# A pair of token tiles closed together, memory rows scaled on GpSimd, and a score reduction moved in its queue: one edit to a two-layer decoder trunk

## The chip, the cores and the metric

The kernel runs on one core of one Trainium2 chip. A core has five engines that each work through a queue of their own in order: TensorE (PE in the profile; PEld is its weight load), VectorE (DVE), ScalarE (ACT), GpSimd (POOL) and SyncE (SP, which here only issues DMAs). The metric is the time of one execution in microseconds: 1540.67 us before (median of three runs, 1540.62 to 1540.80).

## The reference

Two decoder layers over 512 tokens of 1024 channels, all in float32:

```
for l in range(2):
    a = hybrid_mixer(rms_norm(x, pre_mix_g[l]), ...)   # 8 latent (MLA) heads + 8 dilated-window heads
    x = x + rms_norm(a, post_mix_g[l])
    c = memory_cross_attention(rms_norm(x, pre_xattn_g[l]), rms_norm(mem, mem_g[l]), ...)
    x = x + rms_norm(c, post_xattn_g[l])
    h = square(relu(rms_norm(x, pre_mlp_g[l]) @ w_up[l]))
    x = x + rms_norm(h @ w_down[l], post_mlp_g[l])
```

`rms_norm(x, g)` is `x * rsqrt(mean(x*x) + 1e-6) * g` over a row. `mem` is 256 rows of 1024 channels, the same for both layers; the cross attention has 4 heads of 256 channels, the MLP 4096 hidden channels. Softmaxes are causal (latent heads), banded with a bias (dilated heads) or full (memory).

## The kernel before, in words

Tokens lie in four tiles of 128 rows (t = 0 to 3), channels in two halves of 512 (n = 0, 1). `xs[t][n]` is the residual stream. A float32 factor is split into a high part (on ACT) and a low part (on DVE, the difference), and each product is three matmuls: low times high, high times low, high times high (lines 247 to 249). The weights come by DMA into `raw` and are split into `whi` (line 193) and `wlo` (line 199).

A row norm takes four steps on four engines: ACT squares a half and adds it up (`sumsq`, "junk" is its unused output), DVE adds both halves' sums and EPS (a 128x1 tile, `...m`), POOL raises it to the power -1/2 (`rpow`, line 139, `...r`), and then the rows are scaled. For a sub-layer's output (`add_post_norm`, `pnm` and `pnr`) DVE does the last step together with the residual addition (line 432). For the next sub-layer's input (`norm_x`, `n1m` and `n1r` at the layer boundary) POOL scales half 0 into `xn` (line 417) and ACT half 1 (line 414); PE then transposes `xn` through PSUM tiles `tp`, and the result is split into `xth` and `xtl` (line 205).

The order on each engine is made by a scheduler when the program is built: it takes the program order as priorities, and `tc.issue_after(x)` places an instruction behind another. Generators for attention, latent projections and memory work are woven into one stream (`weave`); transposes are put off (`put_off`) so that matmuls can go in front. An instruction that waits holds up all that stands behind it on its engine.

Four places matter here.

- Attention start of a layer. `ev_kd` splits the keys of the dilated heads into `kh` (ACT) and `kl` (DVE, line 663); POOL copies both to the other half of the partitions. `scores` computes a head's scores in four widths, 128 to 512: PE writes `sp`, DVE adds the bias and takes the row minimum into `nm` (line 485), ACT takes the exponent (line 489), POOL divides by the sum (line 491). There are two `sp` buffers, so a third width waits for the reduction of the first. While `pinned[0]` is set, PE's score matmuls are kept in program order, and the first exponent of a head stands behind the last `kh`.
- Memory norm (`memory_norm`): the rows of `mem` (`mr[t][n]`, two tiles of two halves) are normed per tile t, with the scaling on DVE (line 835). It is one of the fills beside the attention heads, once in each layer. PE transposes `mr` later.
- Layer boundary. The MLP's second product runs over seven combinations of quarter matrices (`plan`, as in Winograd's form of Strassen's method); `wa`, `wc` and `we` are their PSUM results, added to `acc[t][n]`. Token tiles 0 and 1 are complete after the fifth combination of the last quarter, tiles 2 and 3 after the last. `done` then takes the sum of squares (`junkp`), multiplies by the gain `gb`, and after a tile's second half calls `add_post_norm` and `norm_x`.
- End of the program. In the last layer tiles 0 and 1 are closed by `finish_by_transfer`: `acc` is scaled (line 1081), a DMA that POOL issues adds the residual `xmid` to it, and SP stores it. Tiles 2 and 3 go through `add_post_norm`, whose `xs` is stored by SP and ACT.

## Time and profile before

| | |
|---|---|
| median of three runs | 1540.67 us (1540.62 to 1540.80) |
| profiled execution | 1540.44 us |
| its span in the trace | 1538.6 us |
| TensorE busy | 1501.9 us, 98% |
| VectorE busy | 985.1 us, 64% |
| ScalarE busy | 821.0 us, 53% |
| GpSimd busy | 253.9 us, 16% |
| chain that ended last | 83% PE, 9% DVE, 3% ACT, 3% issue, 1% POOL |

The span is what the trace covers; 1.8 us of the profiled execution lie outside it. Busy time is summed over an engine's instructions; an engine's idle time costs something only where another engine's end depends on it.

### The profile page before, as it was taken

What the parts mean: (1) busy time and instruction counts of PE and PEld (TensorE: products, weight loads), DVE (VectorE), ACT (ScalarE), POOL (GpSimd) and SP (SyncE); (2) the same over time, 40 slices, a digit from 0 to 9 for tenths busy, and PEclk for the clock granted to TensorE, in tenths of its full rate; (3) what the DMA queues carried; (4) which work ended last, traced back from release to release, by engine and by line L of the source; (5) the groups of instructions that cost most, each with busy time, mean ns of one, the idle gap of its engine ahead of it and who ended that gap; (6) DMA issues with size and microseconds to landing.
All of it is one profiled execution on the core that took longest, in us unless ns stands there. A gap on an engine that the chain in (4) does not pass through costs nothing.

```text
span 1538.6 us, 21318 instructions
## 1 busy us (share of the span) xinstructions
PE 1501.9 (98%) x7861; PEld 1261.4 (82%) x7861; DVE 985.1 (64%) x1768; ACT 821.0 (53%) x1578; POOL 253.9 (16%) x441
## 2 busy tenths in 40 slices
PE   9989999999999999999989999999999999999997
PEld 7777788898898888888868877978988988888885
DVE  5556865456459677684964667654654594958667
ACT  5356665355357364645644666654553654546363
POOL 2143621021020000000111455201111100000002
PEclk9999999999999999999999999999999999999999
DMA  6423223513131505153642322243322324060535
GB/s 235 153 81 105 87 78 103 186 56 123 55 110 56 178 28 182 38 175 97 201 121 64 117 93 73 69 151 137 110 83 69 113 72 158 15 191 28 181 85 117
DMA packets 89581, 168.29 MB, mean 109 GB/s; under 512 B 6358, under 2 KB 12164, under 8 KB 89476
## 3 DMA queue, kind: packets, MB, share of 16 engines
q1 hardware_dynamic: 86436, 161.15, 32.6%
q0 software_dynamic: 2752, 5.24, 2.1%
q8 instruction: 62, 1.02, 0.3%
q10 hardware_dynamic: 288, 0.52, 0.1%
q14 instruction: 43, 0.35, 0.1%
HBM read 158.49 MB, written 11.03 MB: 110 GB/s over the span
## 4 chain that ended last, share of the span: by engine, by line
PE 83%; DVE 9%; ACT 3%; issue 3%; POOL 1%; DMA 1%; SPq 0%; DVEq 0%; POOLq 0%; ACTq 0%
PE pfm L248 12%; PE pfm L247 12%; PE pfm L249 12%; PE ptm L247 6%; PE ptm L249 6%; PE ptm L248 6%; PE wa L247 3%; PE wa L248 3%; PE wa L249 3%; PE sp L481 3%; PE op L238 3%; DVE wlo L199 2%; PE ptp L230 2%; PE wc L248 1%; PE wc L247 1%
## 5 line engine op out<-in xcount | busy, mean ns | idle before, releaser
L248 PE MATMUL pfm<-xth,wlo 128*128 128x512 f32 (+1 forms) x896 | 322.4, 360 | 0.6
L247 PE MATMUL pfm<-xtl,whi 128*128 128x512 f32 (+1 forms) x896 | 322.2, 360 | 0.0
L249 PE MATMUL pfm<-xth,whi 128*128 128x512 f32 (+1 forms) x896 | 321.6, 359 | 0.0
L199 DVE SCALAR_TENSOR_TENSOR wlo<-raw,gT,whi 128x512 fp32r<-128x512 f32 (+3 forms) x332 | 229.5, 728 | 125.1 <-ACT whi L193 123.5
L193 ACT ACTIVATE whi<-raw,gT 128x512 fp32r<-128x512 f32 (+2 forms) x324 | 209.6, 697 | 174.0 <-PE pfm L249 87.3
L248 PEld LDWEIGHTS pfm<-xth,wlo 128*128 128x128 f32 x896 | 169.1, 189 | 26.9 <-DVE wlo L199 1.4
L249 PEld LDWEIGHTS pfm<-xth,whi 128*128 128x128 f32 x896 | 169.1, 189 | 25.5 <-issue 0.5
L247 PEld LDWEIGHTS pfm<-xtl,whi 128*128 128x128 f32 x896 | 169.2, 189 | 25.0
L164 ACT ACTIVATE whi<-raw 128x1024 fp32r<-128x1024 f32 x112 | 118.1, 1059 | 130.5 <-PE pfm L249 54.0
L165 DVE TENSOR_TENSOR wlo<-raw,whi 128x1024 fp32r<-128x1024 f32 x112 | 134.7, 1219 | 39.1 <-ACT whi L164 39.1
L1068 POOL DMA_DIRECT2D raw<-in_w_down x8 | 9.8, 1230 | 596.2 <-DVE raw L1071 540.1
L491 POOL TENSOR_SCALAR P<-P,rs 128x128 f32<-128x128 f32 (+3 forms) x128 | 73.3, 578 | 156.2 <-DVE rs L490 66.6
L247 PE MATMUL wa<-wlo,fh 128*128 128x512 f32 x240 | 93.6, 390 | 0.5 <-DVE acc L1153 0.5
L248 PE MATMUL wa<-whi,fl 128*128 128x512 f32 x240 | 93.4, 389 | 0.0
L249 PE MATMUL wa<-whi,fh 128*128 128x512 f32 x240 | 93.4, 389 | 0.0
L489 ACT ACTIVATE P<-P,nm 128x128 f32<-128x128 f32 (+3 forms) x128 | 71.2, 557 | 24.6 <-DVE nm L485 23.9
L185 DVE TENSOR_TENSOR wlo<-raw,whi 128x1024 fp32r<-128x1024 f32 x32 | 39.1, 1222 | 59.4 <-ACT whi L184 58.6
L247 PE MATMUL ptm<-wlo,xth 128*128 128x512 f32 (+2 forms) x192 | 68.4, 357 | 5.2 <-DVE wlo L199 4.4
L184 ACT ACTIVATE whi<-raw 128x1024 fp32r<-128x1024 f32 x32 | 33.9, 1061 | 67.3 <-PE ptm L249 60.2
L1071 DVE TENSOR_TENSOR raw<-raw 128x1024 f32<-128x1024 f32 x56 | 67.8, 1217 | 0.2
L248 PE MATMUL ptm<-whi,xtl 128*128 128x512 f32 (+2 forms) x192 | 66.5, 346 | 0.2 <-DVE xtl L205 0.2
L249 PE MATMUL ptm<-whi,xth 128*128 128x512 f32 (+2 forms) x192 | 66.5, 346 | 0.0
(253 smaller groups left out, 3257.8 us busy)
## 6 DMA issues: line engine op xcount, KB each, us to landing
raw<-in_w_up SPq DMA_DIRECT2D x64, 512.0 KB, 4.6
raw<-in_w_down SPq DMA_DIRECT2D x64, 512.0 KB, 4.2
raw<-in_w_in SPq DMA_DIRECT2D x24, 512.0 KB, 5.6
raw<-in_w_xk SPq DMA_DIRECT2D x16, 512.0 KB, 4.1
raw<-in_w_xv SPq DMA_DIRECT2D x16, 512.0 KB, 3.7
raw<-in_w_mix_out SPq DMA_DIRECT2D x16, 512.0 KB, 4.1
raw<-in_w_xq SPq DMA_DIRECT2D x16, 512.0 KB, 6.2
raw<-in_w_xo SPq DMA_DIRECT2D x16, 512.0 KB, 3.6
```

The lines of the kernel that those rows point to most:

```text
L164: nc.scalar.activation(hi, raw, AF.Copy)
L165: nc.vector.tensor_sub(lo, raw, hi.bitcast(F32))
L193: weight_parts[:] = [nc.scalar.activation(cols(hi, k, False), cols(raw, k, True), AF.Copy, scale=g).ins]
L199: nc.vector.scalar_tensor_tensor(lv, rv, g, hv, op0=OP.mult, op1=OP.subtract)
L238: nc.tensor.matmul(ps, lhsT=lhsT, rhs=rhs, start=start, stop=stop)
L247: in_order(nc.tensor.matmul(ps, lhsT=lh, rhs=rl, start=first, stop=False, skip_group_check=more))
L248: in_order(nc.tensor.matmul(ps, lhsT=ll, rhs=rh, start=False, stop=False, skip_group_check=more))
L249: in_order(nc.tensor.matmul(ps, lhsT=lh, rhs=rh, start=False, stop=last, skip_group_check=more))
L481: in_order(nc.tensor.matmul(sp[:, :L], lhsT=q[:, i * 128:(i + 1) * 128], rhs=k[:, :L], start=n == 0, stop=n == len(parts) - 1))
L489: nc.scalar.activation(Pi, Pi, AF.Exp, bias=nm[:, i:i + 1], scale=-1.0, accum_out=rs[:, i:i + 1])
L491: nc.gpsimd.tensor_scalar(Pi, Pi, rs[:, i:i + 1], 1.0, op0=OP.mult, op1=OP.mult)
L1071: nc.vector.tensor_add(tile_, tile_, more)
```

## The change

It does four things.

1. The first score reduction of layer 0's first head (DVE) is issued behind the last `kl` subtraction, as the first exponent already was behind the last `kh`.
2. `pinned[0]` is set in layer 0 only; in layer 1 the scheduler orders the attention start freely.
3. The memory norm has one DVE addition (128x2) and one power (128x2) for both tiles, and the four scalings of `mr` go from DVE to POOL.
4. `close_pair` closes tiles 0 and 1 together, once both are complete: one `pnm`, one power, and in layer 0 the four residual additions, one `n1m` and `n1r`, and for each tile one scaling on POOL and one on ACT. In layer 1 it has one power, four scalings of `acc` and the four adding DMAs and stores.

```diff
-    last_key = [None]
+    last_key = [None, None]
...
-            score_op[0] = nc.vector.tensor_tensor_reduce(
-                out=Pi, in0=sp[:, :L], in1=tb[:, 512 - L:512], scale=-scale, scalar=3e38, op0=OP.add,
-                op1=OP.min, accum_out=nm[:, i:i + 1]).ins
+            with tc.issue_after(last_key[1]) if pinned[0] and i == 0 else nullcontext():
+                score_op[0] = nc.vector.tensor_tensor_reduce(
+                    out=Pi, in0=sp[:, :L], in1=tb[:, 512 - L:512], scale=-scale, scalar=3e38, op0=OP.add,
+                    op1=OP.min, accum_out=nm[:, i:i + 1]).ins
...
-                    nc.vector.tensor_sub(lo[here, :], ps[here, :], u[here, :].bitcast(F32))
+                    last_key[1] = nc.vector.tensor_sub(lo[here, :], ps[here, :], u[here, :].bitcast(F32)).ins
...
+            ms = small("mms", 4)
             for t in range(2):
-                ms = small("mms", 2)
                 for n in range(2):
-                    sumsq(mr[t][n], ms[:, n:n + 1], scale=1.0 / 32.0)
-                r = row_rstd((ms[:, 0:1], ms[:, 1:2]), "nm")
+                    sumsq(mr[t][n], ms[:, 2 * n + t:2 * n + t + 1], scale=1.0 / 32.0)
+                yield
+            m = small("nmm", 2)
+            nc.vector.scalar_tensor_tensor(m, ms[:, 0:2], EPS, ms[:, 2:4], op0=OP.add, op1=OP.add)
+            r = rpow(m, "nm")
+            for t in range(2):
                 for n in range(2):
-                    nc.vector.tensor_scalar(mr[t][n], mr[t][n], r[:, 0:1], None, op0=OP.mult)
+                    nc.gpsimd.tensor_scalar(mr[t][n], mr[t][n], r[:, t:t + 1], 1.0, op0=OP.mult, op1=OP.mult)
                 yield
...
-        pinned[0] = True
+        pinned[0] = l == 0
...
-        def finish_by_transfer(t):
-            m = small("pnm", 1)
-            ...
+        def close_pair():
+            v = pair_ss.rearrange("p (t n) -> p t n", t=2)
+            m = small("pnm", 2)
+            nc.vector.scalar_tensor_tensor(m, v[:, :, 0], EPS, v[:, :, 1], op0=OP.add, op1=OP.add)
             r = rpow(m, "pn")
+            if l == DEPTH - 1:
+                for t in range(2):
+                    for n in range(2):
+                        rows, cols = slice(t * 128, (t + 1) * 128), slice(n * 512, (n + 1) * 512)
+                        nc.vector.scalar_tensor_tensor(acc[t][n], acc[t][n], r[:, t:t + 1], gb[n], op0=OP.mult,
+                                                       op1=OP.mult)
+                        nc.gpsimd.dma_start(acc[t][n], xmid[rows, cols], accum_op=OP.add)
+                        nc.sync.dma_start(out[0, rows, cols], acc[t][n])
+                return
+            ms = small("n1ms", 4)
+            for t in range(2):
+                for n in range(2):
+                    nc.vector.scalar_tensor_tensor(xs[t][n], acc[t][n], r[:, t:t + 1], xs[t][n], op0=OP.mult,
+                                                   op1=OP.add)
+                    sumsq(xs[t][n], ms[:, 2 * t + n:2 * t + n + 1], scale=1.0 / 32.0)
+                store_x(t, xsave)
+            v = ms.rearrange("p (t n) -> p t n", t=2)
+            m = small("n1m", 2)
+            nc.vector.scalar_tensor_tensor(m, v[:, :, 0], EPS, v[:, :, 1], op0=OP.add, op1=OP.add)
+            r = rpow(m, "n1")
+            ...
+            for t in range(2):
+                xns = [unit("xn") for _ in range(2)]
+                nc.gpsimd.tensor_scalar(xns[0], xs[t][0], r[:, t:t + 1], 1.0, op0=OP.mult, op1=OP.mult)
+                nc.scalar.activation(xns[1], xs[t][1], AF.Copy, scale=r[:, t:t + 1])
+                put_off(("xt", t), DELAY, lambda t=t, xns=xns: [
+                    transposed(xns[n], n, list(zip(hv, lv)), t) for n in range(2)])
...
-            if ready_halves[t] < 2:
+            if ready_halves[t] < 2 or t == 0:
                 return
-            if by_transfer:
-                finish_by_transfer(t)
+            if t == 1:
+                close_pair()
                 return
```

The order of instructions moves with it. The first place is DVE at layer 0's attention start. Before:

```order
L663 TENSOR_TENSOR kl<-pfm,kh 64x512 x3
L485 ISA P,nm<-sp,tb 128x128
L485 ISA nm 128x1
L663 TENSOR_TENSOR kl<-pfm,kh 64x512 x3
L199 SCALAR_TENSOR_TENSOR wlo<-raw,gT,whi 128x288
L663 TENSOR_TENSOR kl<-pfm,kh 64x512
L199 SCALAR_TENSOR_TENSOR wlo<-raw,gT,whi 128x288 x3
L663 TENSOR_TENSOR kl<-pfm,kh 64x512
L485 ISA P,nm<-sp,tb 128x256
L485 ISA nm 128x1
L485 ISA P,nm<-sp,tb 128x384
```

In the changed kernel:

```order
L664 TENSOR_TENSOR kl<-pfm,kh 64x512 x6
L199 SCALAR_TENSOR_TENSOR wlo<-raw,gT,whi 128x288
L664 TENSOR_TENSOR kl<-pfm,kh 64x512
L199 SCALAR_TENSOR_TENSOR wlo<-raw,gT,whi 128x288 x3
L664 TENSOR_TENSOR kl<-pfm,kh 64x512
L486 ISA P,nm<-sp,tb 128x128
L486 ISA nm 128x1
L199 SCALAR_TENSOR_TENSOR wlo<-raw,gT,whi 128x288 x2
L486 ISA P,nm<-sp,tb 128x256
```

The reduction of the first head's first width (`P,nm<-sp,tb 128x128`) stood behind three of these eight `kl` subtractions and now stands behind all of them; of the `wlo` splits two more stand ahead of the second width.

The second place is DVE at the layer boundary, where tiles 2 and 3 are completed and the first transposed halves (`tp`) are split. Before:

```order
L1157 TENSOR_TENSOR acc<-we,acc 128x512
L385 SCALAR_TENSOR_TENSOR n1m<-n1ms 128x1
L199 SCALAR_TENSOR_TENSOR wlo<-raw,gT,whi 128x512 x2
L1090 TENSOR_TENSOR acc<-acc,gb 128x512
L1157 TENSOR_TENSOR acc<-we,acc 128x512
L1090 TENSOR_TENSOR acc<-acc,gb 128x512 x2
L429 SCALAR_TENSOR_TENSOR pnm<-mss 128x1
L199 SCALAR_TENSOR_TENSOR wlo<-raw,gT,whi 128x512
L432 SCALAR_TENSOR_TENSOR xs<-acc,pnr,xs 128x512 x2
L205 TENSOR_TENSOR xtl<-tp,xth 128x4x128 x2
L385 SCALAR_TENSOR_TENSOR n1m<-n1ms 128x1
L199 SCALAR_TENSOR_TENSOR wlo<-raw,gT,whi 128x512
```

In the changed kernel:

```order
L1187 TENSOR_TENSOR acc<-we,acc 128x512
L1120 TENSOR_TENSOR acc<-acc,gb 128x512
L199 SCALAR_TENSOR_TENSOR wlo<-raw,gT,whi 128x512
L1187 TENSOR_TENSOR acc<-we,acc 128x512
L1120 TENSOR_TENSOR acc<-acc,gb 128x512 x2
L429 SCALAR_TENSOR_TENSOR pnm<-mss 128x1
L205 TENSOR_TENSOR xtl<-tp,xth 128x4x128
L432 SCALAR_TENSOR_TENSOR xs<-acc,pnr,xs 128x512 x2
L205 TENSOR_TENSOR xtl<-tp,xth 128x4x128
L199 SCALAR_TENSOR_TENSOR wlo<-raw,gT,whi 128x512
L385 SCALAR_TENSOR_TENSOR n1m<-n1ms 128x1
L205 TENSOR_TENSOR xtl<-tp,xth 128x4x128
```

The first split `xtl` stood behind the pair of residual additions of tile 2 (`xs`) and now stands ahead of it; of the `wlo` splits of layer 1's first weights fewer stand in front of `pnm` and more behind. Tiles 0 and 1 have their four `xs` in one row further up.

The third place is DVE at the end of the program. Before:

```order
L1155 TENSOR_TENSOR acc<-acc,wc 128x512 x2
L1077 SCALAR_TENSOR_TENSOR pnm<-mss 128x1
L1081 SCALAR_TENSOR_TENSOR acc<-acc,pnr,gb 128x512 x2
L1077 SCALAR_TENSOR_TENSOR pnm<-mss 128x1
L1081 SCALAR_TENSOR_TENSOR acc<-acc,pnr,gb 128x512 x2
L1155 TENSOR_TENSOR acc<-acc,wa 128x512
L1157 TENSOR_TENSOR acc<-wa,acc 128x512
L1155 TENSOR_TENSOR acc<-acc,wa 128x512
L1090 TENSOR_TENSOR acc<-acc,gb 128x512
L1157 TENSOR_TENSOR acc<-wa,acc 128x512
```

In the changed kernel:

```order
L1185 TENSOR_TENSOR acc<-acc,wc 128x512 x2
L1085 SCALAR_TENSOR_TENSOR pnm<-mss 128x2
L1091 SCALAR_TENSOR_TENSOR acc<-acc,pnr,gb 128x512 x4
L1185 TENSOR_TENSOR acc<-acc,wa 128x512
L1187 TENSOR_TENSOR acc<-wa,acc 128x512
L1185 TENSOR_TENSOR acc<-acc,wa 128x512
L1120 TENSOR_TENSOR acc<-acc,gb 128x512
L1187 TENSOR_TENSOR acc<-wa,acc 128x512
L1120 TENSOR_TENSOR acc<-acc,gb 128x512
```

Two pairs of scalings with a sum each became one sum and four scalings; what follows (tiles 2 and 3) is in the same order.

On PE, in the memory norm's stretch, the scores of widths 384 and 512 of one latent head (`sp<-ring`) now follow straight on the transposes `qtp`, ahead of nine matmuls and transposes that stood between them. On POOL the four `mr` scalings stand in two pairs around the division of that head's second width, ahead of its third and fourth. In layer 1's attention start some `ptm` matmuls (input projection) now stand between the widths of a head's scores.

## Rows read from the trace of the kernel before

**Rows 1.** The page, part 1: busy us of engines and weight load, share, instructions.

```profile
PE 1501.9 (98%) x7861; PEld 1261.4 (82%) x7861; DVE 985.1 (64%) x1768; ACT 821.0 (53%) x1578; POOL 253.9 (16%) x441
```

**Rows 2.** Waits of PE: us in total, times, longest us.

```profile
PE sp L481 <- DVE nm L485: 7.2, 15, 1.3
```

**Rows 3.** Stretches: length; busy us (instructions) by engine; PEclk is the granted clock.

```profile
84.00:88.00 4.00, 1.10 (x7) 0.69 (x5) 3.22 (x6) 2.48 (x6) 2.82 (x5) 1.00 0.00 0
...
88.00:92.00 4.00, 3.52 (x12) 2.81 (x12) 3.26 (x11) 3.94 (x9) 3.82 (x5) 0.58 0.50 135
...
776.00:782.00 6.00, 5.21 (x17) 4.39 (x18) 5.28 (x11) 3.23 (x9) 2.40 (x3) 0.54 0.55 184
```

**Rows 4.** Timeline, DVE, layer 0: start us, us, operation, [idle before <-releaser].

```profile
83.69 0.29 DVE L485 CUSTOM_DVE_ANT_0 P<-sp,tb 128x128 f32<-128x128 f32 x1 [9.68 <-PE sp L481]
...
84.02 1.41 DVE L663 TENSOR_TENSOR kl<-pfm,kh 64x512 fp32r<-64x512 f32 x2
...
87.97 1.36 DVE L199 SCALAR_TENSOR_TENSOR wlo<-raw,gT,whi 128x288 fp32r<-128x288 f32 x3
```

**Rows 5.** Timeline, ACT, same place.

```profile
85.47 0.59 ACT L657 ACTIVATE kh<-pfm 64x512 fp32r<-64x512 f32 x1 [6.79 <-DVE kl L663]
...
89.15 1.28 ACT L489 ACT_TABLE_LOAD   x1
```

**Rows 6.** Timeline, PE, same place.

```profile
87.39 0.40 PE L247 MATMUL ptm<-wlo,xth 128*128 128x288 f32 x1 [2.90 <-DVE wlo L199]
```

**Rows 7.** Timeline, PE, layer 1, attention start.

```profile
850.76 0.50 PE L481 MATMUL sp<-kh,qs 128*128 128x512 f32 x1 [1.32 <-DVE nm L485]
```

**Rows 8.** Timeline, DVE, layer 0, memory norm.

```profile
171.43 0.88 DVE L835 TENSOR_SCALAR mr<-mr,nmr 128x512 f32<-128x512 f32 x2 [0.68 <-POOL nmr L139]
...
173.99 1.00 DVE L835 TENSOR_SCALAR mr<-mr,nmr 128x512 f32<-128x512 f32 x2 [0.88 <-POOL nmr L139]
```

**Rows 9.** Timeline, PE, memory norm of layer 0 and of layer 1.

```profile
175.44 0.95 PE L481 MATMUL sp<-ring 96*128 96x512 f32 x3 [0.79 <-DVE nm L485]
...
934.56 0.97 PE L481 MATMUL sp<-ring 96*128 96x512 f32 x3 [0.80 <-DVE nm L485]
```

**Rows 10.** Timeline, POOL, layer 0, memory norm.

```profile
179.68 0.70 POOL L491 TENSOR_SCALAR P<-P,rs 128x512 f32<-128x512 f32 x1
```

**Rows 11.** Timeline, PE, layer boundary.

```profile
772.26 1.18 PE L230 MATMUL tp<-ident,xn 128*128 128x128 f32 x8 [2.71 <-POOL xn L417]
...
776.79 1.09 PE L230 MATMUL tp<-ident,xn 128*128 128x128 f32 x4 [2.41 <-DVE xtl L205]
```

**Rows 12.** Timeline, DVE, layer boundary.

```profile
761.06 0.15 DVE L429 SCALAR_TENSOR_TENSOR pnm<-mss 128x1 f32<-128x1 f32 x1
...
774.63 1.42 DVE L432 SCALAR_TENSOR_TENSOR xs<-acc,pnr,xs 128x512 f32<-128x512 f32 x2 [0.44 <-POOL pnr L139]
```

**Rows 13.** Timeline, POOL, layer boundary.

```profile
761.30 0.94 POOL L139 TENSOR_TENSOR pnr<-pnm,mhalf 128x1 f32<-128x1 f32 x1 [10.15 <-DVE pnm L429]
...
765.75 0.71 POOL L417 TENSOR_SCALAR xn<-xs,n1r 128x512 f32<-128x512 f32 x1
...
770.85 1.32 POOL L417 TENSOR_SCALAR xn<-xs,n1r 128x512 f32<-128x512 f32 x1
```

**Rows 14.** Timeline, ACT, layer boundary.

```profile
771.41 0.58 ACT L381 ACTIVATE junkp<-acc 128x512 f32<-128x512 f32 x1
```

**Rows 15.** Timeline, DVE, end of the program.

```profile
1523.27 1.41 DVE L1081 SCALAR_TENSOR_TENSOR acc<-acc,pnr,gb 128x512 f32<-128x512 f32 x2 [2.00 <-POOL pnr L139]
...
1528.20 0.68 DVE L1157 TENSOR_TENSOR acc<-we,acc 128x512 f32<-128x512 f32 x1
...
1533.92 1.42 DVE L432 SCALAR_TENSOR_TENSOR xs<-acc,pnr,xs 128x512 f32<-128x512 f32 x2 [0.66 <-POOL pnr L139]
```

**Rows 16.** Timeline, PE, end of the program: last matmul for tile 2, and last.

```profile
1525.69 0.39 PE L249 MATMUL we<-whi,fh 128*128 128x512 f32 x1
...
1528.41 0.39 PE L249 MATMUL we<-whi,fh 128*128 128x512 f32 x1
```

More of the change, by code (lines that the diff above doesn't have):

```diff
@@ L1031, in block_kernel @@
         acc = [[None, None] for _ in range(NT)]
-        ss = [small("mss", 2) for _ in range(NT)]
+        pair_ss = small("mss", 4)
+        ss = [pair_ss[:, 0:2], pair_ss[:, 2:4], small("mss", 2), small("mss", 2)]
         nxh = nxl = None
@@ L1072, in right_form @@
             return parts_w(tile_)
-        def finish_by_transfer(t):
-            m = small("pnm", 1)
-            nc.vector.scalar_tensor_tensor(m, ss[t][:, 0:1], EPS, ss[t][:, 1:2], op0=OP.add, op1=OP.add)
+        def close_pair():
+            v = pair_ss.rearrange("p (t n) -> p t n", t=2)
+            m = small("pnm", 2)
+            nc.vector.scalar_tensor_tensor(m, v[:, :, 0], EPS, v[:, :, 1], op0=OP.add, op1=OP.add)
             r = rpow(m, "pn")
-            for n in range(2):
-                rows, cols = slice(t * 128, (t + 1) * 128), slice(n * 512, (n + 1) * 512)
-                nc.vector.scalar_tensor_tensor(acc[t][n], acc[t][n], r[:, 0:1], gb[n], op0=OP.mult, op1=OP.mult)
-                nc.gpsimd.dma_start(acc[t][n], xmid[rows, cols], accum_op=OP.add)
-                nc.sync.dma_start(out[0, rows, cols], acc[t][n])
+            if l == DEPTH - 1:
[18 more added lines that the diff above has]
+            r = rpow(m, "n1")
+            hv = (nxh[:, 0:4, :], nxh[:, 4:8, :])
+            lv = (nxl[:, 0:4, :], nxl[:, 4:8, :])
+            for t in range(2):
[4 more added lines that the diff above has]
+                    transposed(xns[n], n, list(zip(hv, lv)), t) for n in range(2)])
@@ L1085, in done @@
         def done(t, n, junk):
             sumsq(acc[t][n], ss[t][:, n:n + 1], scale=1.0 / 32.0, junk=junk)
-            by_transfer = l == DEPTH - 1 and t < 2
-            if not by_transfer:
+            if l < DEPTH - 1 or t >= 2:
                 nc.vector.tensor_mul(acc[t][n], acc[t][n], gb[n])
             ready_halves[t] += 1
-            if ready_halves[t] < 2:
+            if ready_halves[t] < 2 or t == 0:
                 return
-            if by_transfer:
-                finish_by_transfer(t)
+            if t == 1:
+                close_pair()
```

## The prediction

> **What bounds the kernel.** I read the busy times first: TensorE works 1501.9 us of a span of 1538.6 [rows 1]. What a change can win is in the 36.7 us left, and in stretches where TensorE runs at the lower of its two clock levels. Next the list of TensorE's waits: the largest group, 7.2 us in 15 waits, is scores (`sp`) waiting for DVE's score reductions (`nm`) [rows 2]. Last the timeline of the four places that the change touches. The profiled execution took 1540.44 us, 0.23 less than the median; terms below are differences in that execution's timeline, taken from the median at the end.
>
> **Layer 0's attention start.** DVE stands idle for 9.68 us before the first score reduction, which waits for PE at 83.69, and the `kl` subtractions behind it start at 84.02 [rows 4]. ACT idles 6.79 us, since `kh` at 85.47 waits for the subtraction before it to free a PSUM buffer [rows 5]. The split `wlo` that PE needs comes after them: PE waits 2.90 us until 87.39 [rows 6]. With the reduction moved back this chain of alternating `kh` (0.59) and `kl` (0.70 each) runs while PE is still busy with keys, and the first `wlo` (0.45) is done by some 82: the 2.90 goes.
>
> What is late next: the last pair of `kh` and `kl` cannot start before PE's last key product at 83.5, and three `wlo` stand between (1.36 for three). My walk through the new DVE row: `kl` 84.8, `wlo` 85.3, two more 86.2, last `kl` 86.9, first reduction (0.29) 87.2. PE therefore waits about 0.6 for the second half of that `wlo`. There are two `sp` buffers, so the third width waits until 87.2 (1.2) and the fourth for the second reduction behind two more `wlo` (0.95). The first exponent now stands behind four splits and a table load of 1.28 [rows 5], so the next head's third width waits some 1.6. Together 4.35 us against 4.5 of waits before: the waits change places, and little is won by them.
>
> What is left is the clock. After the 4 us in which PE was busy 1.10, the granted clock was 0.58 over 88 to 92 (1.2 GHz for most of it); PE's 3.52 us busy there would take about 2.0 at the upper level: 1.5 lost [rows 3]. In the new order PE is busy some 1.5 of the same 4 us, in smaller pieces. That is nearer to a fall than to none, but not the same case. Walked on to the transposes of the first head's `P`, PE is there about 0.1 us earlier with the fall and 1.7 without it. I take 0.9, bounds -0.5 and 2.5.
>
> **Layer 1's attention start.** No reduction is pinned here, and PE's widths may be spread. PE's largest wait is 1.32 us for `nm` at 850.76 [rows 7]. With input projection matmuls between the widths, my walk leaves waits of about 0.7 where 1.9 stood, less what shifts behind them: gain 0.8. Bounds: the whole 1.32 won, or as much lost where a projection matmul in front of a score waits for its own split.
>
> **Memory norm, once in each layer.** DVE holds two pairs of `mr` scalings (0.88 and 1.00) and waits 0.68 and 0.88 for the powers ahead of them: 3.4 us ahead of the second score reduction, behind which PE waits 0.79 in layer 0 and 0.80 in layer 1 [rows 8, 9]. Without them both reductions are done about 171.4, when PE issues the two wider scores. I count 0.7 a layer, 1.4 in all; bounds 0.4 and 2.4 (small gaps of PE beside the waits may close too).
>
> The four scalings land on POOL, ahead of the divisions of widths 384 and 512. By the nearest POOL row of that size, 0.70 [rows 10], they take 2.8; the power that is saved goes against it. On my walk the last division ends near 180.8 where it ended at 180.4, and the transposes that read it come near 187: some 6 us cover it. `mr` itself is ready by 177.4 for transposes at 182. So nothing is charged. If the 6 us were gone, each further scaling in front would cost its 0.70.
>
> A POOL scaling of this size does not always take 0.7: at 770.85 `xn` took 1.32, at 765.75 it took 0.71 [rows 13]. The Trainium skill (SBUF — State Buffer, section "Who interferes with whom") says that a VectorE instruction with two SBUF inputs contends with a GpSimd instruction that reads SBUF, and that the later one blocks. DVE ran a product of two SBUF tiles beside the slow one, so the trace agrees; by that rule the scalings could cost 1.32 each, 2.5 us more on POOL, which the 6 us still cover, and the sum would stay as it is.
>
> **Layer boundary.** PE finishes the MLP at 769.5 and waits 2.71 us, until 772.26, for `xn` of tile 1 (POOL done at 772.17, beside ACT's `junkp` from 771.41) [rows 11, 13, 14]. Both tiles' sums were there when DVE began the first `pnm` at 761.06 [rows 12], but they went through in turn. Closed together: second gain product and `pnm` to 761.9, power 0.94 [rows 13] to 762.9, four `xs` (0.71 each, 1.42 a pair [rows 12]) to 765.7, with squares behind each to some 767, sum and power to 768.5, two scalings on ACT and on POOL to 770.0, ACT's `junkp` of tile 2 to 770.8. The first transposes then come near 770.95: 1.3 earlier. With POOL's two at 1.32 they end at 771.2, 1.0 earlier.
>
> The second set of transposes waits 2.41 us for the split `xtl`, which on DVE stood behind the `xs` pair of tile 2 (1.42, after a wait of 0.44 for its power) [rows 11, 12]. Now one `xtl` stands in front: the wait goes. In return three `wlo` of layer 1's first weights stand further back; I walk into new waits of 1.4, about two DVE instructions of 0.7. Sum: 1.3 + 2.4 - 1.4 = 2.3. PE ran at the lower level here too (0.54 over 776 to 782 [rows 3]); I leave that fall in, since PE still works little between 769.5 and 774. Bounds 0.5 and 4.3 (the fall gone: 5.21 busy at 0.54 is worth some 2).
>
> **End of the program.** PE has no wait in its last stretch and ends at 1528.8 [rows 16], so this term comes from DVE. DVE waited 2.00 us for tile 1's power, held on POOL behind two DMA issues, and scaled `acc` from 1523.27; seven instructions later, back to back, `acc<-we` of tile 2 runs at 1528.20, though PE's last matmul for it began at 1525.69 and ended some 0.4 later [rows 15, 16]. The tail follows from it: squares, gain, sum, power, the additions of tile 2, then tile 3, whose last pair starts at 1533.92. With one power the four scalings start near 1520.3 and take 2.7, so the queue is free at 1523.0 instead of 1524.6, and the chain behind moves by 1.6 at most: `acc<-we` at 1526.6 still follows PE's result at 1526.1. The last `acc<-we` cannot come before 1528.8, which it no longer waits long for. I take 1.6, bounds 0.5 (power at 0.94, scalings held up by DMA issues) and 2.0.
>
> **Sum.** 0.9 + 0.8 + 1.4 + 2.3 + 1.6 = 7.0 us. From the median: 1540.67 - 7.0 = 1533.7.
>
> **The rivals.**
>
> *The waits only move* (within 0.2%). For it: at layer 0's start I found 4.35 us of new waits for 4.5 of old ones, and at the boundary 1.4 of new ones. If the boundary's two gains are eaten by late `wlo` splits (2.3 lost), the free order of layer 1 loses 0.5 instead of winning 0.8, and layer 0 wins nothing, then 1533.7 + 2.3 + 1.3 + 0.9 = 1538.2. Against it: the end's term and the memory norm's stand on instructions that leave a queue, and don't depend on this.
>
> *The clock stays up* (faster still). If both falls go, 0.8 more at layer 0 (1.7 instead of 0.9) and 2.0 at the boundary: 1530.9. For it: both falls follow long idle stretches of PE that become shorter. Against: the busy share between is hardly higher.
>
> *The clock stays down* (slower). One long wait turns into four short ones between 84 and 95 and several between 771 and 782, with little work between; if TensorE then runs at the lower level from the first to the last of them, layer 0's some 7 us of work take 7 more, where 1.5 was lost before, and the boundary loses 3 more than the 2 before: 1533.7 + 0.8 + 5.5 + 3.0 = 1543.0. It decides from about 7 us more at the lower level than now, all gains taken together. Against it: elsewhere PE has waits of about 1 us with no fall, as around 850.76 and 175.44 [rows 7, 9].
>
> *The change doesn't do what it says*: the order shows the moved instructions where the code puts them, so this is left out, apart from layer 1, where the scheduler decides; that is in the first rival.
>
> **How the numbers follow.** Forecast 0.60 (own range 1531.5 to 1536.5), clock up 0.17, waits moved 0.16, clock down 0.07. About 0.2%, 3.1 us, is what a measurement of this kernel can tell from no change, so faster means below 1537.6: the forecast, the clock up and a small part of the waits moved, 0.78; the same 0.15; slower 0.07. The range that leaves out 2 in 10 is 1530.0 to 1538.6.
>
> **What would show it.** Layer 0: DVE without the 9.68 us wait, no PE wait of 2.9 us for `wlo`, waits of about 1 us for `nm` in its place, the granted clock of 88 to 92. Layer 1: no wait of 1.3 us. Memory norm: the wait of 0.8 us for `nm` gone in both layers, no new wait of `ptp` for POOL. Boundary: transposes start 1.4 us behind the last `we`, and no wait of 2.4 us for `xtl`. End: `acc<-we` of tile 2 within 1 us of PE's result, and about 8.2 us from the end of PE's last matmul to the end of the span instead of 9.8. Wrong it would be if PE waits for POOL's divisions or if the four places together give back less than 3 us.

## The result, and the profile after

The changed kernel takes 1529.63 us (median of four runs, 1527.39 to 1531.26) against 1540.74 for the kernel before on the same chip (1540.62 to 1541.41). The ratio is 0.9926, with an interval of 0.9909 to 0.9943: 11.1 us faster. The forecast was 1533.7. The time lies 0.4 us below the low end of the range that leaves out 2 in 10 (1530.0), and 1.9 below that of the forecast's own range (1531.5).

The profiled execution was the slowest of the four, 1531.26 us with a span of 1529.5. I look first at the page's busy times and at TensorE's longest waits, as in [rows 1, 2].

The page of the changed kernel, part 1:

```profile
PE 1500.9 (98%) x7861; PEld 1262.2 (83%) x7861; DVE 983.7 (64%) x1755; ACT 820.6 (54%) x1578; POOL 254.1 (17%) x444
```

TensorE's work is the same 7861 matmuls and 1.0 us less of busy time, so 8.1 of the 9.1 us by which the span is shorter were idle time. The waits of PE in the changed kernel (us in total, times, longest us):

```profile
PE sp L481 <- DVE nm L486: 5.1, 11, 1.0
PE ptm L247 <- DVE wlo L199: 2.0, 2, 1.5
PE tp L230 <- POOL xn L417: 1.6, 1, 1.6
...
PE tp L230 <- ACT junkp L381: 1.1, 1, 1.1
...
PE tp L230 <- POOL pnr L139: 0.8, 1, 0.8
```

The waits for score reductions went from 7.2 us in 15 to 5.1 in 11. The longest waits for `wlo` (1.5) and for `xn` (1.6) stand at 15.59 and 7.35, in the program's start, which the change does not touch. To see where the rest came from, I matched the same matmul ahead of and behind each place in both traces, and took by how much TensorE gained between the two:

| place | forecast | changed kernel, profile of 1531.26 | the same kernel run again, profile of 1527.74 |
|---|---|---|---|
| layer 0, attention start | 0.9 | 0.85 | 2.63 |
| memory norm, layer 0 | 0.7 | 1.86 | 1.88 |
| layer boundary | 2.3 | 2.70 | 3.52 |
| layer 1, attention start | 0.8 | 1.87 | 1.85 |
| memory norm, layer 1 | 0.7 | 1.87 | 1.86 |
| end, behind PE's last matmul | 1.6 | 0.54 | 0.64 |
| sum | 7.0 | 9.7 | 12.4 |
| difference of the spans | | 9.1 | 12.6 |

The last two lines differ, among other things, by the program's first microseconds: at 50 to 70 us the profiled kernels stand between 1.2 us behind the kernel before (x12) and 0.6 ahead of it (x5). Tails are good to about 0.05 us, since spans are given to 0.1.

**Layer 0's attention start.** TensorE's timeline in the changed kernel (start us, us, operation, idle before and its releaser; beside [rows 6]):

```profile
85.61 0.40 PE L247 MATMUL ptm<-wlo,xth 128*128 128x288 f32 x1 [0.48 <-DVE wlo L199]
...
87.52 0.44 PE L481 MATMUL sp<-kh,qs 128*128 128x384 f32 x1 [1.01 <-DVE nm L486]
...
89.08 0.80 PE L481 MATMUL sp<-kh,qs 128*128 128x512 f32 x1 [0.83 <-DVE nm L486]
```

The wait of 2.90 us for `wlo` is gone, and three shorter ones stand in its place, as walked (0.6, 1.2 and 0.95 were forecast); the fourth of the walk, 1.6 for the next head's third width, does not appear in this profile. The reduction that DVE had waited 9.68 us for [rows 4] now runs at once at 87.17:

```profile
87.17 0.29 DVE L486 CUSTOM_DVE_ANT_0 P<-sp,tb 128x128 f32<-128x128 f32 x1
```

What decides the gain here is the clock. Stretches of the profile of 1531.26 (length; busy us and instructions of PE, PEld, DVE, ACT, POOL; granted clock; DMA), beside [rows 3]:

```profile
84.00:88.00 4.00, 2.51 (x16) 1.89 (x14) 3.50 (x9) 3.95 (x9) 3.32 (x4) 0.98 0.25 65
88.00:92.00 4.00, 3.17 (x11) 2.74 (x11) 3.16 (x11) 3.88 (x10) 1.09 (x3) 0.50 0.64 214
92.00:96.00 4.00, 4.00 (x21) 3.74 (x21) 2.21 (x12) 1.87 (x7) 2.97 (x8) 0.66 0.56 180
```

PE was busy 2.51 us of the first 4 where it was busy 1.10 before, and yet it fell to the lower level (0.50, 1.2 GHz) for longer: (0.02 + 0.50 + 0.34) of 4 us, times two, is 6.9 us at that level (6.8 by the finer stretches used below), against 3.4 by the same working in the kernel before.

**Memory norm.** TensorE in layer 0, beside [rows 9]:

```profile
169.71 0.62 PE L481 MATMUL sp<-ring 96*128 96x128 f32 x4
...
170.97 1.47 PE L481 MATMUL sp<-ring 96*128 96x384 f32 x6
...
176.01 2.37 PE L238 MATMUL op<-PT,vd 128*64 128x512 f32 x14
...
180.69 0.86 PE L481 MATMUL sp<-ring 96*128 96x128 f32 x6
```

The scores of widths 384 and 512 now run as one row of six matmuls without the wait of 0.79. The same stretch of work, from one row of narrow scores to the next, in the kernel before:

```profile
170.28 0.62 PE L481 MATMUL sp<-ring 96*128 96x128 f32 x4
...
182.72 0.86 PE L481 MATMUL sp<-ring 96*128 96x128 f32 x6
```

GpSimd takes the scalings as walked:

```profile
173.52 1.36 POOL L840 TENSOR_SCALAR mr<-mr,nmr 128x512 f32<-128x512 f32 x2
...
175.31 1.37 POOL L840 TENSOR_SCALAR mr<-mr,nmr 128x512 f32<-128x512 f32 x2
...
179.47 0.69 POOL L492 TENSOR_SCALAR P<-P,rs 128x512 f32<-128x512 f32 x1
```

Each costs about 0.7, and the last division ends at 180.2 where it ended at 180.4 [rows 10]; no transposes wait for it.

**Layer boundary.** TensorE, beside [rows 11]:

```profile
768.43 1.18 PE L230 MATMUL tp<-ident,xn 128*128 128x128 f32 x8 [1.05 <-ACT junkp L381]
770.05 0.51 PE L247 MATMUL ptm<-wlo,xth 128*128 128x512 f32 x1 [0.44 <-ACT xth L203]
771.36 1.09 PE L230 MATMUL tp<-ident,xn 128*128 128x128 f32 x4 [0.81 <-POOL pnr L139]
```

The waits of 2.71 and 2.41 became 1.05 and 0.81. DVE's split `xtl` stands ahead of the `xs` pair of tile 2, beside [rows 12]:

```profile
770.53 0.68 DVE L205 TENSOR_TENSOR xtl<-tp,xth 128x512 fp32r<-128x512 f32 x1
771.29 1.41 DVE L432 SCALAR_TENSOR_TENSOR xs<-acc,pnr,xs 128x512 f32<-128x512 f32 x2
```

**Layer 1's attention start.** Stretches of equal length that begin at the same work, first of the changed kernel, then of the kernel before (columns as above):

```profile
840.00:865.00 25.00, 24.92 (x171) 22.09 (x170) 18.09 (x57) 18.68 (x50) 12.03 (x29) 1.00 0.33 103
```

```profile
845.00:870.00 25.00, 22.91 (x160) 20.07 (x159) 16.26 (x55) 17.00 (x47) 12.35 (x29) 1.00 0.28 86
```

Nearly all idle time there went, the 1.32 of [rows 7] and two shorter waits (0.57 and 0.20), and no new one came; the same 25 us hold 171 matmuls where they held 160.

**End of the program.** DVE, beside [rows 15]; PE's last matmul begins at 1519.85 and lasts 0.39:

```profile
1512.03 2.74 DVE L1091 SCALAR_TENSOR_TENSOR acc<-acc,pnr,gb 128x512 f32<-128x512 f32 x4 [0.85 <-POOL pnr L139]
...
1524.01 1.42 DVE L432 SCALAR_TENSOR_TENSOR xs<-acc,pnr,xs 128x512 f32<-128x512 f32 x2 [0.66 <-POOL pnr L139]
```

DVE's chain ends 5.19 us behind PE (1525.43 against 1520.24), where it ended 6.54 behind before. The span, though, ends 9.26 us behind PE where it ended 9.80 behind.

### The profile page after: what moved, and what is told of

The parts are those of the page before. It is cut to its first block, busy times and chain, and to the rows that moved or that the text cites. A ratio compares the mean times of both kernels' runs of the same rounds, so it can differ in the third digit from the quotient of the medians.

```text
span 1529.5 us, 21301 instructions
## 1 busy us (share of the span) xinstructions
PE 1500.9 (98%) x7861; PEld 1262.2 (83%) x7861; DVE 983.7 (64%) x1755; ACT 820.6 (54%) x1578; POOL 254.1 (17%) x444
## 3 DMA queue, kind: packets, MB, share of 16 engines
q8 instruction: 62, 1.02, 0.3%
## 4 chain that ended last, share of the span: by engine, by line
PE 85%; DVE 8%; ACT 3%; issue 2%; POOL 1%; DMA 1%; SPq 0%; DVEq 0%; POOLq 0%; ACTq 0%
PE pfm L248 12%; PE pfm L247 12%; PE pfm L249 12%; PE ptm L247 7%; PE ptm L249 7%; PE ptm L248 7%; PE sp L481 3%; PE wa L247 3%; PE wa L249 3%; PE wa L248 3%; PE op L238 3%; DVE wlo L199 2%; PE ptp L230 2%; PE wc L249 1%; PE wc L247 1%
```

## The experiments

Three questions were open: what the memory norm really holds, what the clock adds, and why the end gives less than its chain. In the table "gain" is taken as in the table above, in us of each kernel's profiled execution against that of before (a minus is a loss), and "lower level" is the time at 1.2 GHz at layer 0's start (80 to 112 us) and at the boundary (755 to 795), worked out from the granted clock of the stretches. The last column is the time from PE's last matmul to the end of the span.

| kernel | layer 0 start | memory l0 | boundary | layer 1 start | memory l1 | lower level | tail |
|---|---|---|---|---|---|---|---|
| before | | | | | | 3.4 / 6.8 | 9.80 |
| changed | 0.85 | 1.86 | 2.70 | 1.87 | 1.87 | 6.8 / 6.8 | 9.26 |
| x1 changed, again | 2.63 | 1.88 | 3.52 | 1.85 | 1.86 | 0 / 0 | 9.16 |
| x2 reduction behind the keys | 2.63 | 0 | -0.45 | -0.34 | 0 | 0 / 10.2 | |
| x3 layer 1 free | -1.01 | 0 | 0.17 | 1.99 | 0 | 6.8 / 6.8 | |
| x4 memory norm | -0.12 | 1.85 | 0.24 | 0 | 1.88 | 6.8 / 6.8 | |
| x5 one power, DVE scales | -0.73 | 1.17 | 0.22 | 0 | 1.17 | 6.8 / 6.8 | |
| x6 two powers, POOL scales | 0 | 1.52 | 0.77 | 0 | 1.58 | 3.4 / 6.8 | |
| x7 pair closed | -0.08 | 0 | 3.56 | 0 | 0 | 6.8 / 0 | 9.08 |
| x8 pair closed at the end only | -0.33 | 0 | 0.97 | 0 | 0 | 6.8 / 6.8 | 8.80 |
| x9 fill | 2.63 | 1.87 | 3.54 | 1.87 | 1.90 | 0 / 0 | 8.77 |
| x10 last stores | 1.86 | 1.82 | 2.74 | 1.87 | 1.90 | 3.4 / 6.8 | 8.61 |
| x11 all but memory norm | 1.85 | 0 | 3.56 | 1.99 | 0 | 3.4 / 0 | 8.86 |
| x12 layer 0 free too | 2.8 | 1.87 | 3.54 | 1.99 | 1.88 | 3.4 / 3.4 | 9.16 |
| x13 fill and last stores | 2.62 | 1.84 | 3.53 | 1.87 | 1.87 | 0 / 0 | 8.65 |

**x1: the changed kernel again.** No edit.

> The changed kernel once more. Clock theory: its runs spread over 4 us (1527.4 to 1531.3) because the granted clock falls for a different length in each run, at layer 0's attention start and at the layer boundary, while PE's waits stay the same; then the fast runs again lie between 1527 and 1532, and this profile shows the same waits as the first (1.0 and 0.8 us for nm at layer 0, 1.1 and 0.8 us of tp at the boundary) with another length of the stretch at 0.5. Rival, that the order's waits themselves vary (DMA landing): the waits differ by over 1 us somewhere and the clock stretches are equal.

Measured: 1528.47 us (1527.68 to 1529.35), ratio 0.9913 (0.9900 to 0.9927). The granted clock of the whole span was 0.998 in the two runs of 1527.7 and 0.995 and 0.996 in those of 1529.2 and 1529.35. The profile of 1527.74 shows no fall at either place, though PE did the same work there: this execution runs 0.48 us earlier, and over the stretch that answers to 84 to 88 PE was busy 2.50 us, against 2.51 where the clock then fell. The next head's third width now waits 0.69:

```profile
83.52:87.52 4.00, 2.50 (x16) 1.89 (x14) 3.49 (x9) 3.95 (x9) 3.32 (x4) 1.00 0.23 57
87.52:91.52 4.00, 2.92 (x19) 2.48 (x18) 3.65 (x13) 3.88 (x10) 1.58 (x3) 1.00 0.73 221
```

```profile
92.06 0.44 PE L481 MATMUL sp<-kh,qs 128*128 128x384 f32 x1 [0.69 <-DVE nm L486]
```

So the clock falls in some executions of one and the same program and not in others, and the step at layer 0 is worth 0.85 or 2.63 by that alone. The memory norm and layer 1 don't move with it.

**x2: the first part alone.**

```diff
+            with tc.issue_after(last_key[1]) if pinned[0] and i == 0 else nullcontext():
                 score_op[0] = nc.vector.tensor_tensor_reduce(
...
```

> The kernel before with edit 1 alone (first score reduction behind the last kl in layer 0). From the trace of after: 0.9 us at this place with a fall of the clock of over 6 us, up to 3.9 if the fall goes; time 1537 to 1540, about 1539.5. Rival, that the waits only move: 1540.2 to 1541. In either case the 2.9 us wait of ptm for wlo is gone, two waits of about 1 us for nm are there, and layer 1, the memory norm and the boundary stand as before.

Measured: 1540.31 us (1538.14 to 1541.60), ratio 0.9988 (0.9979 to 0.9997). Its profiled execution took 1538.35: layer 0 gains 2.63 without a fall, and the boundary, with 10.2 us at the lower level, gives 0.45 back. The reordering at layer 0 does work without the other parts; it is worth little on the median. The edit is not quite the first part alone: `pinned[0]` is still set in layer 1 here, so the reduction is moved back there too, and PE's two waits for `nm` of 1.32 and 0.57 became 1.34 and 0.86, about the 0.34 lost at layer 1's start.

**x3: the second part alone.**

```diff
-        pinned[0] = True
+        pinned[0] = l == 0
```

> The kernel before with edit 2 alone (layer 1's attention start ordered freely). The trace of after showed 1.9 us there against 0.8 predicted: if that is this edit's, 1538.8 and the shift stands between 845 and 865 of the timeline. Rival, that part of it came from edit 4 in layer 1 or from an earlier end of other work: 1539.9 (0.8) or less won. No other place should move.

Measured: 1539.65 us (1537.68 to 1541.44), ratio 0.9990 (0.9981 to 0.9999). Layer 1's start gains 1.99, with the same stretch as in the changed kernel, shown here for x3:

```profile
846.00:871.00 25.00, 24.91 (x171) 22.14 (x170) 18.12 (x57) 18.70 (x51) 12.44 (x29) 1.00 0.33 101
```

In this execution layer 0, which is not edited, lost 1.01 in a longer fall (6.8 us instead of 3.4), and its first microseconds 0.6, which is why its span is only 0.4 us shorter.

**x4: the third part alone.**

```diff
-                r = row_rstd((ms[:, 0:1], ms[:, 1:2]), "nm")
...
-                    nc.vector.tensor_scalar(mr[t][n], mr[t][n], r[:, 0:1], None, op0=OP.mult)
+                    nc.gpsimd.tensor_scalar(mr[t][n], mr[t][n], r[:, t:t + 1], 1.0, op0=OP.mult, op1=OP.mult)
```

> The kernel before with edit 3 alone (one power and four scalings on GpSimd in both memory norms). Theory after the result: this is the mis-sized term, 1.9 us in each layer against 0.7 predicted; then 1536.9, with steps of 1.8 to 1.9 us at both places. As predicted: 1539.3. Rival, that edits 1 and 4 shifted the stretch and helped: between the two, with unequal steps.

Measured: 1537.79 us (1536.35 to 1538.50), ratio 0.9973 (0.9963 to 0.9984). The places gain 1.85 and 1.88, 3.7 in all, where I had counted 1.4. This is the term that was mis-sized, and it needs none of the other parts.

**x5: one power, the scalings still on DVE.**

```diff
-                    nc.gpsimd.tensor_scalar(mr[t][n], mr[t][n], r[:, t:t + 1], 1.0, op0=OP.mult, op1=OP.mult)
+                    nc.vector.tensor_scalar(mr[t][n], mr[t][n], r[:, t:t + 1], None, op0=OP.mult)
```

(against x4)

> The kernel before with half of edit 3: one sum and one power for both memory tiles, the four scalings still on DVE. Theory A (the scalings on DVE hold up the score reductions and the splits behind them, and moving them off is the gain): most of the 1.86 us a layer is missing, at most 0.5 is won, time within 1 us of before. Theory B (the two powers one behind the other, each waited for by DVE, are the loss, and the matmul order that follows from it): 1 us or more a layer, 1537 to 1539.

Measured: 1538.26 us (1537.67 to 1540.52), ratio 0.9982 (0.9973 to 0.9991); 1.17 at each place. One power alone brings the two wide scores together, and a wait for `ring` is left in its trace, the split that now stands behind the scalings on DVE:

```profile
175.44 0.63 PE L230 MATMUL ptp<-ident,P 128*128 128x128 f32 x4 [0.23 <-DVE ring L205]
```

**x6: two powers, the scalings on POOL.**

```diff
-                    nc.vector.tensor_scalar(mr[t][n], mr[t][n], r[:, 0:1], None, op0=OP.mult)
+                    nc.gpsimd.tensor_scalar(mr[t][n], mr[t][n], r[:, 0:1], 1.0, op0=OP.mult, op1=OP.mult)
```

(against before)

> The kernel before with the other half of edit 3: two sums and two powers as before, the scalings on GpSimd. Theory A: 1.4 us or more of the 1.86 a layer, 1537 to 1538.5. Theory B: under 0.7 a layer, 1539.5 or later. In the order PE's two wider scores come a few matmuls later than with one power, so a part (0.3) may be missing under either.

Measured: 1537.90 us (1536.95 to 1539.52), ratio 0.9980 (0.9971 to 0.9989); 1.52 and 1.58 at the places. So neither half is the whole and neither is nothing: 1.17 and 1.52 add to 2.69, more than the 1.86 of both. Each takes the same chain (power, then scalings, then the second reduction) out of DVE's queue ahead of that reduction, and the second half to come finds most of it gone.

**x7: the fourth part alone.**

```diff
+            if t == 1:
+                close_pair()
                 return
...
```

> The kernel before with edit 4 alone (pair closed at the layer boundary and at the end). From the trace of after: 2.7 us at the boundary where the clock falls as long as before, 3.5 where it doesn't fall, 0.5 at the end; 1536.5 to 1538.5, about 1537.5. As predicted: 2.3 + 1.6, 1537.0. Rival, that the boundary needed the other edits: under 1.5 there.

Measured: 1536.13 us (1535.70 to 1538.06), ratio 0.9970 (0.9958 to 0.9982). The boundary gains 3.56 with no fall, and the tail 0.7. By its places the pair closing is the largest part of the change, though 0.8 of the 3.56 is the fall that is absent here (2.70 with it in the changed kernel); by its time it can't be told from the third part.

**x8: the pair closed at the end of the program only.**

```diff
+            pair = l == DEPTH - 1
+            if ready_halves[t] < 2 or pair and t == 0:
+                return
+            if pair and t == 1:
+                close_pair()
+                return
...
```

> The kernel before with edit 4 in the last layer only (one power, four scalings of acc); the layer boundary as before. The chain on DVE from the scalings to the last residual addition ends 1.3 to 1.4 us earlier against PE's last matmul (5.1 us before, 3.8 after), but the span only about 0.5, if the stores behind it are held by the adding DMAs, which now run four in a row: 1540.0 to 1540.4 and the last stores issued right behind those of tiles 0 and 1. If the 1.6 of the prediction were lost elsewhere in the changed kernel, the whole 1.3 shows here: 1539.3.

Measured: 1539.56 us (1538.41 to 1543.01), ratio 0.9991 (0.9983 to 1.0000). DVE's chain ends 5.20 us behind PE, 1.34 earlier than before, but the span only 1.0. The boundary, whose code is that of before, shows a gain of 0.97 with a fall as long as before. The fall lies earlier against the work here: it has begun when the first eight transposes run, which took 1.18 before [rows 11], and more of it lies over waits that follow:

```profile
773.70 1.63 PE L230 MATMUL tp<-ident,xn 128*128 128x128 f32 x8 [2.70 <-POOL xn L417]
```

x6 shows the same (1.35 for these transposes, a gain of 0.77), and x3, x4 and x5, where they take 1.18, gain 0.2. So a place that no edit touches can move by 1 us with where a fall lies.

**x9: work in layer 0's waits.** Score matmuls of the first head are repeated into the same buffer (widths 256 and 384), some 1.7 us of added TensorE work; nothing is left out.

```diff
+        fill = {1: 4, 2: 2} if pinned[0] and not filled[0] else {}
...
+            for _ in range(fill.get(i, 0)):
+                for n, (q, k) in enumerate(parts):
+                    in_order(nc.tensor.matmul(sp[:, :L], ...))
```

> The changed kernel, with the first head's score matmuls of width 256 issued four more times and those of width 384 twice more in layer 0 (same result written again, 1.7 us of matmuls), where PE otherwise waits 1.0 and 0.8 us for nm. Clock theory (PE's idle share at this place decides whether the clock falls, and the spread of the changed kernel comes from it): no fall at layer 0 in the profile, the shift at that place 2.4 to 2.7 us against the kernel before, and the runs lie between 1527 and 1529.5 with a spread that only the boundary makes. Rival (the falls come from outside and do not follow PE's work): a fall here again, runs from 1527.4 to 1531.5 as before. If the added matmuls are not hidden, 0.5 to 1.7 us later than the changed kernel.

Measured: 1528.72 us (1527.32 to 1529.25), ratio 0.9918 (0.9904 to 0.9931). No fall at layer 0, and the granted clock is 0.997 or 0.998 in all five runs:

```profile
84.00:88.00 4.00, 3.45 (x22) 2.77 (x20) 3.94 (x10) 3.93 (x9) 3.42 (x4) 1.00 0.40 87
88.00:92.00 4.00, 3.07 (x20) 2.71 (x20) 3.65 (x17) 3.66 (x12) 1.97 (x4) 1.00 0.59 192
```

The filling cost PE nothing at the place (2.63, as in x1). Of the eight runs of the changed kernel five were at 0.996 or less. With x13, nine of nine runs with the filling are at 0.997 or more, against three of eight without it, which speaks for the theory that the idle time decides; one profile each doesn't show it, since x1 and x2 had no fall there without the filling. The median still can't be told from that of the changed kernel, so what the clock costs it on the median is small.

**x10: the last stores on ACT's queue.**

```diff
-                (nc.sync, nc.scalar)[n].dma_start(dst[t * 128:(t + 1) * 128, n * 512:(n + 1) * 512], xs[t][n])
+                nc.scalar.dma_start(dst[t * 128:(t + 1) * 128, n * 512:(n + 1) * 512], xs[t][n])
```

> The changed kernel, with the last stores of tiles 2 and 3 issued all by ScalarE, so that none stands in SyncE's queue behind the stores of tiles 0 and 1, which wait for the adding DMAs. If SyncE's queue holds back the end: the time from PE's last matmul to the end of the span 8.5 to 8.9 us instead of 9.3, and 0.4 to 0.8 us off the median. Rival (the DMA engines are busy with the earlier stores in any case): 9.2 to 9.5 and no difference.

Measured: 1529.09 us (1528.74 to 1529.76), ratio 0.9921 (0.9909 to 0.9934); tail 8.61. In the changed kernel the stores of tiles 0 and 1 hold SyncE's queue until just before the first store of `xs`, as its timeline shows (SPq is the queue):

```profile
1517.50 5.62 SPq L1094 DMA_DIRECT2D out_x<-acc  x4
1523.21 1.92 SPq L434 DMA_DIRECT2D out_x<-xs  x2
```

With ACT issuing the last stores the tail is the shortest measured (8.61, and 8.65 in x13, against 8.77 to 9.26 for the others with the pair), but a few tenths are less than the runs of one kernel differ by. The last stores, of tile 3, are not held by the queue: SyncE's last issue ends at 1525.13, 0.30 ahead of the end of DVE's chain, as in the kernel before (1535.03 against 1535.34):

```profile
1531.95 3.08 SPq L434 DMA_DIRECT2D out_x<-xs  x2
```

What is late is tile 2's first store, some 1.2 us behind its `xs`, and what is longer is the time from the end of DVE's chain to the end of the span: 3.3 us before, 4.05 in the changed kernel, 3.5 in x10 and in x13. Whether the late store or the other transfers lengthen it stays open.

**x11: all but the third part.** The memory norm is that of before, the rest is changed (against the changed kernel):

```diff
-            r = rpow(m, "nm")
...
-                    nc.gpsimd.tensor_scalar(mr[t][n], mr[t][n], r[:, t:t + 1], 1.0, op0=OP.mult, op1=OP.mult)
+                r = row_rstd((ms[:, 0:1], ms[:, 1:2]), "nm")
...
+                    nc.vector.tensor_scalar(mr[t][n], mr[t][n], r[:, 0:1], None, op0=OP.mult)
```

> The changed kernel with edit 3 undone (the memory norm as before). If the two memory norms give 1.86 each here too, without any share of the other edits, the steps at both places are 0 and the time is 3.7 us above the changed kernel's, 1532 to 1533.5. If what I predicted (0.7 each) were right inside the changed kernel: 1530.

Measured: 1532.48 us (1531.60 to 1533.97), ratio 0.9943 (0.9931 to 0.9956): 4.0 us more than x1's median, and both memory places gain nothing. The old wait is back:

```profile
172.49 0.34 PE L247 MATMUL ptm<-wlo,ch 128*128 128x384 f32 x1
172.68 0.34 PE L248 MATMUL ptm<-whi,cl 128*128 128x384 f32 x1
173.78 0.97 PE L481 MATMUL sp<-ring 96*128 96x512 f32 x3 [0.77 <-DVE nm L486]
```

So the third part is worth the same with the other parts and without them.

**x12: layer 0 left free as well.**

```diff
-        pinned[0] = l == 0
+        pinned[0] = False
```

> The changed kernel with no pinning in layer 0 either, so that both layers' attention starts are ordered freely and edit 1's placing drops out. If free order by itself is what wins 1.9 us in layer 1, layer 0 wins at least 1 us more and the time is 1526.5 to 1528. If it is what stands on DVE ahead of the key splits (in this order the first two score reductions stand ahead of four kl subtractions, as in the kernel before), the idle time of DVE is back, the first wlo is late, and layer 0 loses 1 to 3 us: 1529.5 to 1532.

Measured: 1527.74 us (1526.88 to 1529.20), ratio 0.9909 (0.9893 to 0.9926), not to be told from the changed kernel. DVE's long wait is back, without harm, and another one comes instead. DVE, then PE, of x12:

```profile
85.03 0.29 DVE L486 CUSTOM_DVE_ANT_0 P<-sp,tb 128x128 f32<-128x128 f32 x1 [9.80 <-PE sp L481]
```

```profile
90.14 1.44 PE L230 MATMUL ptp<-ident,P 128*128 128x128 f32 x4 [1.52 <-POOL P L492]
```

My reading of [rows 4 to 6], that the reduction at the head of DVE's queue is what makes PE wait, is therefore too narrow: where projection matmuls with finished splits stand between the scores, PE runs on while DVE catches up.

**x13: x9 and x10 together.** Both diffs above in one kernel.

> The changed kernel with both the added matmuls of x9 and the stores of x10. If SyncE's queue held back the end: PE's last matmul to the end of the span 8.5 to 8.7 us as in x10, no fall of the clock at layer 0 as in x9, and the median 0.3 to 0.6 under the changed kernel's 1528.5. If the end varies with the DMAs whatever the queue: 8.6 to 9.3 and the same time, 1528.3 to 1529.

Measured: 1527.68 us (1527.39 to 1528.51), ratio 0.9912 (0.9897 to 0.9926), clock 0.997 to 0.999. No version is shown to beat the changed kernel; x13, x12 and x1 lie within 0.8 us of each other (x12 and x13 ran on another chip than x1), and the intervals of their ratios overlap.

The four parts alone save 0.12, 0.10, 0.27 and 0.30%, 0.79% together; all at once save 0.74 and 0.87% in two series. Within their intervals they add up.

## Why the prediction was right or wrong

**Memory norm: the step that failed, by its size.** "I count 0.7 a layer" measured 1.82 to 1.90 in every kernel that has the whole part, with the others (x1, x9) or alone (x4), and nothing where it is undone (x11): 3.7 in all against 1.4, and above my upper bound of 2.4. That is 2.3 us of the 4.1 by which the forecast fell short. Of the rest, layer 1 gave 1.1, the boundary 0.4 with a fall and 1.2 without, layer 0 nothing with the long fall and 1.7 without, and the end took about 1 back. The mechanism stood (x5 and x6 each show a part of it): DVE no longer holds the second reduction up, POOL's scalings cost 0.7 each, and their cover held. I had priced one row, the wait of 0.79, rounded down. From the traces: the stretch from 170.28 to 182.72 before took 12.44 us, the same work after, 169.71 to 180.69, took 10.98, so 1.46 was won there and the other 0.4 in smaller waits just behind. A recorded wait also costs a little more than its figure: in the row of x11 above, 173.78 follows 172.68 by 1.10, while the next matmul starts 0.19 (172.49 and 172.68) to 0.28 later (172.88 and, of the scores, 173.16 in the kernel before) when nothing waits. So the wait of 0.77 cost 0.8 to 0.9, and that of 0.79 before 0.85 to 0.95. The remaining 0.5 to 0.6 is in PE's busy time: over the two stretches PE's busy time went from 11.59 us to 10.92 and its idle time from 0.85 to 0.06. I read it from the order: PE changes less often between kinds of matmul (the two wide scores in one row of 1.47 instead of rows of 0.79 and 0.95, fourteen `op` in one row). No run isolates that.

**Layer 1: right in kind, 1.1 us too small.** The walk left waits of 0.7 where 1.9 stood. The scheduler left none (x3: 1.99). My upper bound took in only the largest wait; the others recorded there (0.57 and 0.20) went too.

**Layer boundary: right.** Both gains came where they were walked: transposes behind ACT's `junkp`, 1.05 us after the last `we`, and `xtl` ahead of `xs`. With the fall left in, the forecast was 2.3 and 2.70 was measured; 3.5 without it.

**Layer 0: near by luck.** 0.9 was forecast with a fall like that of before (3.4 us). With a fall of that length the place gives 1.85 (x10, x11), and without one 2.63; 0.85 came with one of 6.8. The walk put 4.35 us of new waits against 4.5 of old ones. Recorded are 4.0 before and 3.1 in x1 (0.48, 1.02, 0.94 and 0.69): the fourth wait, 1.6 on paper, is 0.69, and it is gone where the matmuls ahead of it run at the lower level. PE was also busier there than walked, 2.51 us of the 4 and not 1.5. What I took for a choice between two cases is a difference between executions of one kernel.

**The rival "the clock stays up"** came true in part of the runs. It added 0.8 and 2.0 us; measured are 0.8 at layer 0 against a fall of 3.4 us (1.8 against one of 6.8) and 0.8 at the boundary. How much a fall costs hangs on where it lies: the boundary of x12 gives 3.54 with 3.4 us at the lower level, no less than without a fall. In the profiles of the seven kernels without the first part, layer 0's start shows a fall each time; with it in force, none in x1, x2, x9 and x13 and 3.4 to 6.8 us in the changed kernel's first profile, x10 and x11 (in x12, where nothing is pinned, it has no effect: 3.4). At the boundary, no kernel without the pair closing was seen free of a fall; with it five profiles were (x1, x7, x9, x11, x13). "The clock stays down" was not seen as a loss of that size, though x2 shows its kind (10.2 us at the boundary). "The waits only move" came true at no place of the changed kernel: each of them gained.

**End: too large by about 1 us.** The chain on DVE moved by 1.35 of the 1.6, but I took the end of that chain for the end of the program. Behind it stand the last stores. They are issued at the same distance from the chain's end as before, but from there to the end of the span it takes 4.05 us and not 3.3 (3.5 to 4.05 in the kernels with the pair). The four adding DMAs now leave in a row, with the stores of tiles 0 and 1 behind them; whether these slow the last stores is not shown. Of 9.8 us, 9.3 remain and not 8.2.

**POOL beside DVE: right.** The `mr` scalings ran at 0.68 to 0.70 each, three of the four beside DVE instructions that read one of their tensors from PSUM. At the boundary it is the other case. POOL, then DVE, of the changed kernel:

```profile
766.41 1.79 POOL L1111 TENSOR_SCALAR xn<-xs,n1r 128x512 f32<-128x512 f32 x2
```

```profile
766.64 1.00 DVE L1120 TENSOR_TENSOR acc<-acc,gb 128x512 f32<-128x512 f32 x1
767.56 1.17 DVE L199 SCALAR_TENSOR_TENSOR wlo<-raw,gT,whi 128x512 fp32r<-128x512 f32 x1
768.66 0.68 DVE L1187 TENSOR_TENSOR acc<-we,acc 128x512 f32<-128x512 f32 x1
```

The two scalings take 1.79 instead of 1.36, and DVE's two instructions on SBUF tiles 1.00 and 1.17 while they run (0.68 and 0.74 elsewhere, at 1516.48 and 773.22); the addition from PSUM (`we`) behind them takes 0.68. The Trainium skill (SBUF — State Buffer, section "Who interferes with whom") says that a VectorE instruction with two SBUF inputs contends with a GpSimd instruction that reads SBUF, and that one with at most one SBUF input, outside its two-port modes, does not. The trace agrees at both places. It shows that both sides take longer where the instructions alternate.

## What to carry to other kernels

Price a freed queue by the whole stretch (from the last matmul that did not wait to the next long run without waits), not by the one wait that the list shows: here the stretch held more than twice as much. When a chain is shortened at the end of a program, ask what is issued behind it, since the stores behind it keep a time of their own (3.3 us here before, 3.5 to 4.05 after). And where TensorE is idle a few microseconds at a time, compare several executions of one kernel before a change of the clock is credited to an edit, and compare stretches that hold the same work.

## What the runs showed of the hardware

The length of a fall of TensorE's clock differs between executions of the same program: 6.8 us at layer 0 in one profile of the changed kernel and none in another, with PE busy 2.51 and 2.50 of 4 us over the same work ahead of it. Its cost differs with where it lies: two falls of 6.8 us at the layer boundary, in kernels whose code there is the same, cost 0.97 us more in the kernel before than in x8. GpSimd's power of a 128x2 tile took 0.70 to 0.72 us against 0.54 to 0.57 for 128x1, but 1.16 at 759.73 beside a split `wlo` on DVE (0.99 for 128x1 in the same case, at 769.76 in the kernel before), so a doubled power is nearly free and its neighbour is not.
